# A decoder layer on one core: the held prefetch at the second residual, split first casts, PSUM tiles and stores at the end

## The chip, the cores and the metric

The kernel runs on one core of one Trainium2 chip. The metric is the device time of one execution in microseconds (us). Before the change it is 2006.1 us, the median of three runs between 2005.92 and 2006.18. PE is TensorE, DVE is VectorE, ACT is ScalarE, POOL is GpSimd and SP is SyncE, whose queue issues nearly all DMAs here.

## What is computed

One hybrid decoder layer on 256 tokens of width 2048 in float32: two token mixers side by side (retention and an RG-LRU), merged by gates; cross-attention to 256 memory tokens; a gated FFN of width 5632 with a causal convolution; and a last RMS norm. Cut to the steps around the change:

```python
h = h + merged @ w_mix_out                       # first residual
hn = rmsnorm(h, norm_xa_w)
h = h + memory_cross_attention(hn, mem_n, ...)   # ends with o @ xa_w_o: second residual
hn = rmsnorm(h, norm_ffn_w)
up = causal_dwconv(hn @ ffn_w_up, conv_w, conv_b)
gate, val = jnp.split(up, 2, axis=-1)
h = h + (silu(gate) * val) @ ffn_w_down          # third residual
return rmsnorm(h, final_norm_w)
```

## The kernel before, in words

**Products.** Every float32 product is made of three PE passes over operands that are each split into a rounded part hi and a rest lo (hi x hi, lo x hi, hi x lo). Activations stand by feature in tiles `s` (both parts side by side), so they are PE's stationary operand; weights are the moving operand, 512 columns wide. A product has 16 tiles of 128 rows of weights (k-tiles), taken in chunks of four (KC), and two halves of 128 tokens each. A chunk is thus 4 x 2 x 3 = 24 matmuls of 128x512. PE keeps the order of the program (L221).

**The weight stream.** The host lays all weights out in the order of use. `prefetch(n)` (L237) takes chunks from this stream until n are ahead: it requests a chunk from SP into a tile `raw` (three buffers), ACT casts it to `hi` (L283) and DVE subtracts to get `lo` (L284), two k-tiles at a time, into six buffers each. `chunks` (L296) calls `prefetch(AHEAD)` with AHEAD = 2 after it has taken each chunk, and then runs what `later` has put off by a number of chunks. The tile framework's scheduler then orders the instructions of each engine; what is marked `keep_in_program_order` keeps its place among the marked. The first ten chunks are the interleaved chunks of two products (EARLY = 2, 2, 4, 4, 4 k-tiles each), whose requests are marked. In front of them stand WARM matmuls on a tile of ones (L218).

**Turning rows.** A product gives rows by token, and the next product needs them by feature. `by_dma` (L364) copies rows to 16-bit planes on ACT (L372, one copy for each half of the tokens), turns each with a transposing DMA on SP (L373), and puts off a `join` by some chunks, in which ACT joins the planes again (L383). `split_cols` (L425) then scales by the norm weight and splits into hi and lo (L429 on ACT, L430 on DVE).

**The second residual.** `residual` (L792) makes four column blocks of the product with xa_w_o. The first two are interleaved. For each block DVE adds the accumulator to the rows of h (L804), and `by_dma` turns them (L805), with a wait of one chunk for all but the second. The FFN's first gate product follows at once; its chunk i needs the turned block i.

**The end.** `down` (L949) adds the last FFN product. Its last block goes through `last_down` (L964): the first 128 tokens are made in one accumulator of 512 columns, the second in two pieces of 256 columns, in the unused halves of two accumulator tiles. Each half's sums of squares go to POOL for a power (L998, L1000), then DVE and ACT scale four blocks and four stores of 256 KB each leave, three from SP and one from ACT (L1001 to L1012).

Of the kernel before, what the change touches and what calls it, by code (L numbers as in the profile page):

```python
# [31 lines left out]
RAW_BUFS = 3  # L32
PART_BUFS = 6
AHEAD = 2
WARM = 8
FREE = 300
RG_WAIT = 3
EPS = 1e-6
# [98 lines left out]
def hybrid_layer(  # L137
# [96 lines left out]

    at = [0]

    def prefetch(n):  # L237
        while len(ahead) < n and taken[0] < len(stream):
            i = taken[0]
            name, row, nk, c = stream[i]  # L240
            taken[0] += 1
            size = nk * P * BW
            src = wall[at[0] : at[0] + size].rearrange("(p k n) -> p k n", p=P, k=nk)
            at[0] += size
            if i < 4:
                raw = big([P, KH, BW], s="raw")
            else:
                raw = wp.tile([P, KC, BW], F32, tag="raw", bufs=RAW_BUFS, name=nm("raw"))
            k2 = row // (KH * P)
            early = i < 2 * len(EARLY)  # L250
            own = early and i % 2 == 0
            cuts = range(nk + 1) if i == 0 else range(0, nk + 1, KH) if i < 6 else (0, nk)
            if own:
                xs.load(k2 + 1)
            for a, b in zip(cuts, cuts[1:]):
                load(raw[:, a:b, :], src[:, a:b, :], early)
                if i == 0 and a == 0:
                    load(*xs.rest, early)
                elif own and a == 0:
                    xs.load(k2 + nk // KH)  # L260
            if i >= 6:
                load_x(min(4, 2 * i - 11))
            if i == 8:
                load(cid, consts[:, 0:C_DEC], True)
                load(pa[:, 16:P], by_feature[:, 16:P], True)
                load(pb, by_feature[:, P : P + 80], True)
            if i == 13:
                load(pf.rearrange("p a n -> p (a n)"), by_feature[:, P + 80 :], True)
            if i in (8, 9):
                for b in (2 * i - 16, 2 * i - 15):  # L270
                    sum_squares(xin[b], ss0, b)
            parts = []
            for k in range(0, nk, KH):
                if own:
                    xs[k2 + k // KH]
                hi = wp.tile([P, KH, BW], F32R, tag="hi", bufs=PART_BUFS, name=nm("hi"))
                lo = wp.tile([P, KH, BW], F32R, tag="lo", bufs=PART_BUFS, name=nm("lo"))
                for cs in (slice(k, k + 1), slice(k + 1, k + 2)) if i < 2 else (slice(k, k + KH),):
                    ds = slice(cs.start - k, cs.stop - k)
                    if i == 0:  # L280
                        dve.tensor_copy(hi[:, ds], raw[:, cs, :])
                    else:
                        act.copy(hi[:, ds], raw[:, cs, :])  # L283
                    dve.tensor_tensor(  # L284
                        out=lo[:, ds], in0=raw[:, cs, :], in1=hi[:, ds].bitcast(F32), op=ALU.subtract
                    )
                parts.append((hi, lo))
            ahead.append(((row, c), parts))
# [7 lines left out]
    def chunks(nk, w, row, c):  # L296

        i = gemms[0]
        assert plan[i] == (w, row, nk, c), (i, w, row, nk, c)
        gemms[0] += 1  # L300
        for k, n in pieces(i, nk):
            prefetch(1)
            (r_, c_), parts = ahead.pop(0)
            assert (r_, c_) == (row + k * P, c)
            prefetch(AHEAD)
            yield k, n, parts
            step[0] += 1
            due = [p for p in pending if p[0] <= step[0]]
            pending[:] = [p for p in pending if p[0] > step[0]]
            for _, fn in due:  # L310
                fn()

    def ended(steps):

        for a in steps:
            pass
        return a
# [43 lines left out]

        return t[:, j, cs], t[:, j, S + cs.start : S + cs.stop]

    def by_dma(rows, then, wait=1):  # L364


        planes = big([P, 2, 2, BW], U16, s="pl")
        turned_ = big([P, 2, 4, S], U16, s="pt")
        words = rows.bitcast(U16).rearrange("p t (n h) -> p t h n", h=2)
        for tt in range(2):  # L370
            with tc.high_priority(FREE):
                act.copy(planes[:, tt], words[:, tt])  # L372
            sp.dma_start_transpose(  # L373
                out=turned_.rearrange("p h f s -> p (h f) s")[:, :, tt * P : (tt + 1) * P],
                in_=planes[:, tt].rearrange("p h n -> p (h n)"),
            )

        def join():
            f = big([P, 4, S], s="f")
            halves_ = f.bitcast(U16).rearrange("p f (s h) -> p h f s", h=2)  # L380
            for tt in range(2):
                cs = slice(tt * P, (tt + 1) * P)
                act.copy(halves_[:, :, :, cs], turned_[:, :, :, cs])  # L383
            then(f)

        later(wait, join)
# [405 lines left out]
    def residual(w, st, out, wcol, steps=None):  # L792

        ss = sums()
        products = [steps_n(w, 0, st, NT, b * BW) for b in range(4)]
        for b in range(4):
            if steps:
                steps(b)
            if b == 0:
                for one in products[:2]:  # L800
                    for _ in range(NT // KC - 1):
                        next(one)
            h = hrow[b]
            dve.tensor_add(h, h, ended(products[b]))  # L804
            by_dma(h, lambda f, b=b: turn(f, b, out, wcol), 1 + (b == 1))  # L805
            if b < 2:
                later(2 + b, lambda h=h, b=b: squares(h, ss, b))
            else:
                squares(h, ss, b)
        return ss  # L810
# [153 lines left out]
    def last_down(b0, hid, n, b):  # L964

        h = hrow[b]
        half = sp_.tile([P, 1], F32, tag="half", bufs=1, name="half")
        dve.memset(half, 0.5)
        accs = [acc(), acc()]
        parts = [p for _, _, ps in chunks(n, "ffn_w_down", b0 * BW, b * BW) for p in ps]  # L970

        def total(o, tt, cs):
            for k in range(n):
                hi, lo = (t[:, k % KH, cs] for t in parts[k // KH])
                for _ in products_n(o, hid[k // 2][:, k % 2, :], hi, lo, tt, k == 0, k == n - 1):
                    pass

        for tt in range(2):
            last = big([P, BW + 1], s="last")
            before = sp_.tile([P, 1], F32, tag="pt3", bufs=2, name=nm("pt3"))  # L980
            if tt == 0:
                total(accs[0][:, 0, :], tt, slice(0, BW))
            for c in range(2):
                cs = slice(c * S, (c + 1) * S)
                o = accs[c][:, 1, 0:S] if tt else accs[0][:, 0, cs]
                if tt:
                    total(o, tt, cs)
                y = last[:, c * S : (c + 1) * S + c]
                dve.tensor_add(last[:, cs], h[:, tt, cs], o)  # L989
                junk = tp.tile([P, S + 1], F32, tag="tr", bufs=2, name=nm("junk"))  # L990
                dve.scalar_tensor_tensor(  # L991
                    out=junk[:, 0 : S + c], in0=y, scalar=1.0 / D if c else 1.0, in1=y, op0=ALU.mult, op1=ALU.mult,
                    accum_out=ss3[:, tt, b + c : b + c + 1],
                )
                if c == 0:
                    dve.tensor_reduce(out=before, in_=ss3[:, tt, 0:4], axis=AX.X, op=ALU.add)
                    dve.tensor_scalar_add(before, before, EPS * D)
                    pool.tensor_tensor(out=last[:, BW : BW + 1], in0=before, in1=half, op=ALU.pow)  # L998
            r = sp_.tile([P, 1], F32, tag="ro", bufs=5, name=nm("ro"))
            pool.tensor_tensor(out=r, in0=ss3[:, tt, 4:5], in1=mhalf[:, 0:1], op=ALU.pow)  # L1000
            for c in (1, 0, 3, 2):  # L1001
                y = hrow[c][:, tt, :]
                if c == 3:
                    dve.scalar_tensor_tensor(
                        out=y, in0=last[:, 0:BW], scalar=r, in1=wfin[1][:, 1, :], op0=ALU.mult, op1=ALU.mult
                    )
                elif c == 1:
                    dve.tensor_scalar_mul(y, y, r)
                else:
                    act.mul(y, y, r)  # L1010
                queue = act if c == 2 else sp
                queue.dma_start(out=out[0, tt * P : (tt + 1) * P, c * BW : (c + 1) * BW], in_=y)  # L1012

    ss3 = sp_.tile([P, 2, 5], F32, tag="ss3", bufs=1, name="ss3")

# [60 lines left out]
```

## Time and profile before

| | us |
|---|---|
| median of 3 runs | 2006.1 |
| runs | 2005.92, 2006.10, 2006.18 |
| profiled execution, its own time | 2006.16 |
| its span, first to last instruction | 2004.2 |
| mean granted TensorE clock | 0.999 |

The span of the profiled execution is 1.96 us shorter than its own time; what lies around the span is not on the profile. A row of the timeline has the start from the span's beginning, the time taken, engine and line, the operation, the tiles written and read, and in brackets how long the engine had been idle and what released it. A row of the chain of waits has start, length and what the time went to; "DMA raw<-in_wall" is a weight load under way. "SPq" is the issue of a DMA by SP. The view of windows lists for each stretch the busy time of each engine with its count, then the granted clock, the DMA share and GB/s.

### The profile page before, as it was taken

How to read it: one execution, taken by the hardware profiler on the slowest of the kernel's cores; microseconds unless marked ns; L12 is line 12 of the kernel's file. 1: busy time of each engine (PE TensorE's matmuls, PEld its weight loads, DVE VectorE, ACT ScalarE, POOL GpSimd, SP SyncE). 2: the span in 40 equal slices, each digit the busy share in tenths (PEclk: the TensorE clock that was granted, in tenths of full speed). 3: DMA queues.
4: the chain of work that ended last, by engine and by line, in shares of the span. 5: the costliest groups of instructions: out<-in, count | busy, mean ns of one | idle time of the engine just before them, and what ended most of it. 6: DMA issues, size and time to landing. Idle time of an engine off the chain costs nothing.

```text
span 2004.2 us, 23312 instructions
## 1 busy us (share of the span) xinstructions
PE 1993.6 (99%) x8924; PEld 1656.2 (83%) x8924; DVE 1268.9 (63%) x1566; ACT 1270.2 (63%) x1499; POOL 8.8 (0%) x14
## 2 busy tenths in 40 slices
PE   9999999999999999999999999999999999999998
PEld 7888888888888888888888888888888888888887
DVE  6857756888545555566555654667764576754775
ACT  6646548988444555587666666767763577734763
POOL 0000000000000000000000000000000000000000
PEclk9999999999999999999999999999999999999999
DMA  8755657665655556777666567767665577655673
GB/s 328 238 209 172 237 200 206 214 210 179 218 199 192 199 198 212 268 256 241 203 217 211 193 198 206 213 202 226 231 212 194 179 227 229 204 207 202 205 239 119
DMA packets 197904, 425.58 MB, mean 212 GB/s; under 512 B 142240, under 2 KB 146848, under 8 KB 152736
## 3 DMA queue, kind: packets, MB, share of 16 engines
q1 hardware_dynamic: 197360, 423.55, 64.3%
q8 instruction: 70, 1.15, 0.2%
q10 hardware_dynamic: 432, 0.53, 0.1%
q14 instruction: 42, 0.34, 0.0%
HBM read 388.39 MB, written 2.10 MB: 195 GB/s over the span
## 4 chain that ended last, share of the span: by engine, by line
PE 98%; DMA 1%; DVE 0%; ACT 0%; issue 0%; SPq 0%; POOLq 0%; POOL 0%
PE acc L222 96%; PE sm L222 2%; DMA pt<-pl 0%; DMA raw<-in_wall 0%; DVE lo L284 0%; ACT hi L283 0%; SPq L192 0%; ACT pl L372 0%; ACT nat L1010 0%; DVE last L989 0%; DVE nat L804 0%; ACT junk L822 0%; POOLq L1072 0%; POOL last L998 0%; DVE junk L991 0%
## 5 line engine op out<-in xcount | busy, mean ns | idle before, releaser
L222 PE MATMUL acc<-hi,s 128*128 128x512 f32 x5720 | 1757.7, 389 | 1.2 <-DVE last L989 0.8
L222 PEld LDWEIGHTS acc<-hi,s 128*128 128x128 f32 x5720 | 1071.7, 188 | 222.0 <-DVE last L989 1.3
L284 DVE TENSOR_TENSOR lo<-raw,hi 128x1024 fp32r<-128x1024 f32 (+1 forms) x714 | 859.7, 1220 | 596.9 <-ACT hi L283 579.4
L222 PE MATMUL acc<-lo,s 128*128 128x512 f32 x2860 | 1110.0, 388 | 0.5 <-DVE lo L284 0.5
L283 ACT CAST hi<-raw 128x1024 fp32r<-128x1024 f32 (+1 forms) x712 | 734.5, 1050 | 469.4 <-PE acc L222 427.3
L222 PEld LDWEIGHTS acc<-lo,s 128*128 128x128 f32 x2860 | 537.0, 188 | 112.1 <-DVE lo L284 1.3
L383 ACT COPY f<-pt 128x1024 uint16<-128x1024 uint16 x128 | 168.9, 1353 | 99.9 <-DMA pt<-pl 99.9
L372 ACT COPY pl<-rows 128x1024 uint16<-128x1024 uint16 x100 | 99.7, 1045 | 55.2 <-DVE rows L396 42.9
L396 DVE TENSOR_SCALAR rows<-acc,ro 128x512 f32<-128x512 f32 x76 | 53.4, 744 | 6.2 <-PE acc L222 6.2
L917 DVE SCALAR_TENSOR_TENSOR fg<-f,pf,fg 128x255 f32<-128x255 f32 (+1 forms) x88 | 37.4, 479 | 29.7 <-ACT fg L915 29.3
L917 DVE SCALAR_TENSOR_TENSOR fv<-f,pf,fv 128x255 f32<-128x255 f32 (+1 forms) x88 | 36.1, 478 | 3.9 <-ACT fv L915 3.8
L915 ACT ACTIVATE fg<-f,pf 128x256 f32<-128x256 f32 x44 | 22.9, 592 | 0.3
L915 ACT ACTIVATE fv<-f,pf 128x256 f32<-128x256 f32 x44 | 23.1, 592 | 0.0
L729 DVE SCALAR_TENSOR_TENSOR xr<-f,pa,xr 128x255 f32<-128x255 f32 (+2 forms) x48 | 20.2, 480 | 3.4 <-ACT xr L727 3.3
L404 DVE TENSOR_TENSOR s<-f,s 128x512 fp32r<-128x512 f32 x24 | 15.5, 687 | 9.9 <-ACT s L403 9.9
L430 DVE SCALAR_TENSOR_TENSOR s<-f,pb,s 128x256 fp32r<-128x256 f32 x48 | 20.1, 480 | 2.2 <-ACT s L429 2.2
L372 ACT COPY pl<-nat 128x1024 uint16<-128x1024 uint16 x16 | 15.9, 1045 | 7.5 <-DVE nat L804 7.5
L429 ACT ACTIVATE s<-f,pb 128x256 fp32r<-128x256 f32 x48 | 20.6, 503 | 0.0
L222 PEld LDWEIGHTS sm<-s,s 128*128 128x128 f32 x144 | 18.8, 191 | 0.9
L222 PE MATMUL sm<-s,s 128*128 128x256 f32 (+1 forms) x144 | 18.6, 279 | 0.0
L935 ACT ACTIVATE ft<-fg 128x512 f32<-128x512 f32 x22 | 13.9, 632 | 7.3 <-DVE fg L917 7.3
L418 ACT ACTIVATE v<-acc,ro 128x512 fp32r<-128x512 f32 x16 | 11.0, 686 | 10.2 <-DVE v L419 10.2
(137 smaller groups left out, 561.3 us busy)
## 6 DMA issues: line engine op xcount, KB each, us to landing
raw<-in_wall SPq DMA_DIRECT2D x352, 1024.0 KB, 4.9
nat<-in_x SPq DMA_DIRECT2D x8, 512.0 KB, 8.7
raw<-in_wall SPq DMA_DIRECT2D x7, 512.0 KB, 8.6
pt<-pl SPq DMA_TRANSPOSE x128, 3.3
nat<-in_mem SPq DMA_DIRECT2D x4, 512.0 KB, 8.4
xt<-in_x_t SPq DMA_DIRECT2D x3, 512.0 KB, 10.2
xt<-in_mem_t SPq DMA_DIRECT2D x3, 512.0 KB, 4.9
out<-nat SPq DMA_DIRECT2D x6, 256.0 KB, 2.9
```

Of the source, the lines that this page charges most:

```text
L222: tc.keep_in_program_order(pe.matmul(*a, **k))
L283: act.copy(hi[:, ds], raw[:, cs, :])
L284: dve.tensor_tensor(out=lo[:, ds], in0=raw[:, cs, :], in1=hi[:, ds].bitcast(F32), op=ALU.subtract)
L372: act.copy(planes[:, tt], words[:, tt])
L383: act.copy(halves_[:, :, :, cs], turned_[:, :, :, cs])
L396: dve.tensor_scalar_mul(rows[:, tt, :], a[:, tt, :], r[:, tt : tt + 1])
L404: dve.tensor_tensor(out=t[:, :, S:BW], in0=src, in1=t[:, :, 0:S].bitcast(F32), op=ALU.subtract)
L429: act.activation(t[:, j, 0:S], src[:, j, :], AF.Identity, scale=wcol(j))
L430: dve.scalar_tensor_tensor(out=t[:, j, S:BW], in0=src[:, j, :], scalar=wcol(j), in1=t[:, j, 0:S].bitcast(F32), op0=ALU.mult, op1=ALU.subtract,
L729: dve.scalar_tensor_tensor(out=y[:, s:S], in0=z[:, 0 : S - s], scalar=p_cw(3 - s, t), in1=y[:, s:S], op0=ALU.mult, op1=ALU.add,)
L915: act.activation(y, z[:, j, :], AF.Identity, scale=pf[:, 2, t : t + 1], bias=pf[:, 3, t : t + 1])
L917: dve.scalar_tensor_tensor(out=y[:, s:S], in0=z[:, j, 0 : S - s], scalar=pf[:, 2 - s, t : t + 1], in1=y[:, s:S], op0=ALU.mult, op1=ALU.add,)
```

## The change

There are four edits in one.

1. The start: one warm matmul less; the first weights are requested ahead of the first x; four chunks of the stream instead of two are cast and subtracted one k-tile at a time.
2. The second residual's last block: the chunks up to the last are taken first, then, while `held` is set, the last chunk is taken without a prefetch; its two transposing DMAs are marked to keep their order; then the prefetch runs, its request marked as well.
3. The last product's second half gets two accumulator tiles of its own.
4. The end: the scaling by the last norm weight is taken out of the last step; DVE and ACT write into a tile of 4 x 512 columns, which leaves in two stores of 512 KB from SP.

```diff
-WARM = 8
+WARM = 7
...
+    held = [False]
+
+    def prefetch(n, pin=False):
...
-            if own:
+            if own and i > 0:
                 xs.load(k2 + 1)
             for a, b in zip(cuts, cuts[1:]):
-                load(raw[:, a:b, :], src[:, a:b, :], early)
+                load(raw[:, a:b, :], src[:, a:b, :], early or pin)
                 if i == 0 and a == 0:
+                    xs.load(1)
                     load(*xs.rest, early)
...
-                for cs in (slice(k, k + 1), slice(k + 1, k + 2)) if i < 2 else (slice(k, k + KH),):
+                for cs in (slice(k, k + 1), slice(k + 1, k + 2)) if i < 4 else (slice(k, k + KH),):
...
-            prefetch(AHEAD)
+            if not held[0]:
+                prefetch(AHEAD)
...
-    def by_dma(rows, then, wait=1):
+    def by_dma(rows, then, wait=1, pin=False):
...
-            sp.dma_start_transpose(
+            turning = sp.dma_start_transpose(
...
+            if pin:
+                tc.keep_in_program_order(turning)
...
+            hold = b == 3 and steps is None
+            if hold:
+                for _ in range(NT // KC - 1):
+                    next(products[b])
+            held[0] = hold
             dve.tensor_add(h, h, ended(products[b]))
-            by_dma(h, lambda f, b=b: turn(f, b, out, wcol), 1 + (b == 1))
+            by_dma(h, lambda f, b=b: turn(f, b, out, wcol), 1 + (b == 1), hold)
+            if hold:
+                held[0] = False
+                prefetch(AHEAD, True)
...
-        accs = [acc(), acc()]
+        accs = [acc() for _ in range(3)]
...
-                o = accs[c][:, 1, 0:S] if tt else accs[0][:, 0, cs]
+                o = accs[1 + c][:, 0, 0:S] if tt else accs[0][:, 0, cs]
...
+                dve.tensor_tensor(out=last[:, cs], in0=last[:, cs], in1=wfin[1][:, 1, cs], op=ALU.mult)
             r = sp_.tile([P, 1], F32, tag="ro", bufs=5, name=nm("ro"))
             pool.tensor_tensor(out=r, in0=ss3[:, tt, 4:5], in1=mhalf[:, 0:1], op=ALU.pow)
-            for c in (1, 0, 3, 2):
...
-                queue.dma_start(out=out[0, tt * P : (tt + 1) * P, c * BW : (c + 1) * BW], in_=y)
+            scaled = wp.tile([P, 4, BW], F32, tag="raw", bufs=RAW_BUFS, name=nm("out"))
+            rows = [hrow[c][:, tt, :] for c in range(3)] + [last[:, 0:BW]]
+            for c in range(2):
+                dve.tensor_scalar_mul(scaled[:, 2 * c, :], rows[2 * c], r)
+                late = S if c else 0
+                act.mul(scaled[:, 2 * c + 1, late:], rows[2 * c + 1][:, late:], r)
+                if late:
+                    dve.tensor_scalar_mul(scaled[:, 3, 0:late], rows[3][:, 0:late], r)
+                sp.dma_start(
+                    out=out[0, tt * P : (tt + 1) * P, 2 * c * BW : 2 * (c + 1) * BW],
+                    in_=scaled[:, 2 * c : 2 * c + 2, :].rearrange("p c n -> p (c n)"),
+                )
```

More of the change, by code (lines that the diff above doesn't have):

```diff
@@ L235, in hybrid_layer @@
     at = [0]
-    def prefetch(n):
+    held = [False]
+    def prefetch(n, pin=False):
         while len(ahead) < n and taken[0] < len(stream):
@@ L998, in last_down @@
                     pool.tensor_tensor(out=last[:, BW : BW + 1], in0=before, in1=half, op=ALU.pow)
+                dve.tensor_tensor(out=last[:, cs], in0=last[:, cs], in1=wfin[1][:, 1, cs], op=ALU.mult)
             r = sp_.tile([P, 1], F32, tag="ro", bufs=5, name=nm("ro"))
             pool.tensor_tensor(out=r, in0=ss3[:, tt, 4:5], in1=mhalf[:, 0:1], op=ALU.pow)
-            for c in (1, 0, 3, 2):
[L1002 to L1011, printed above, removed]
-                queue.dma_start(out=out[0, tt * P : (tt + 1) * P, c * BW : (c + 1) * BW], in_=y)
+            scaled = wp.tile([P, 4, BW], F32, tag="raw", bufs=RAW_BUFS, name=nm("out"))
[10 more added lines that the diff above has]
+                )
     ss3 = sp_.tile([P, 2, 5], F32, tag="ss3", bufs=1, name="ss3")
```

## The prediction

> **What bounds the kernel now.** I read the page first, then the waits of PE, then the chain of waits from its end, and last the timeline at the places where the chain leaves PE. Two rows of the page, of its part 1 and its part 4:
>
> ```profile
> PE 1993.6 (99%) x8924; PEld 1656.2 (83%) x8924; DVE 1268.9 (63%) x1566; ACT 1270.2 (63%) x1499; POOL 8.8 (0%) x14
> ...
> PE 98%; DMA 1%; DVE 0%; ACT 0%; issue 0%; SPq 0%; POOLq 0%; POOL 0%
> ```
>
> PE is busy for 99% of the span and carries 98% of the chain, so an edit matters only where PE stands still, before its first matmul or after its last. The change keeps every matmul of the product and their order. The chain of waits shows where PE is left:
>
> ```profile
> 3.55 6.33 DMA raw<-in_wall
> ...
> 9.90 1.06 ACT hi L283
> ...
> 10.98 1.24 DVE lo L284
> ...
> 1112.79 161.66 PE acc L222 x713
> ...
> 1275.55 1.23 DVE lo L284
> 1276.78 1.14 DVE nat L804
> ...
> 1292.92 693.70 PE acc L222 x3059
> ...
> 1987.45 4.58 PE acc L222 x36
> ```
>
> Three places: the start (until 12.3), the end of the second residual (1276 to 1293), and the last product (before 1987.45). The row of 713 matmuls gives the pitch of PE, 161.66/713 = 0.2267 us; a chunk of four k-tiles is 24 matmuls, 5.44 us. The timeline of PE prices the three gaps:
>
> ```profile
> 11.04 0.70 PE L222 MATMUL acc<-hi,s 128*128 128x512 f32 x2
> 12.27 0.50 PE L222 MATMUL acc<-lo,s 128*128 128x512 f32 x1 [0.53 <-DVE lo L284]
> ...
> 1292.17 0.39 PE L222 MATMUL acc<-hi,s 128*128 128x512 f32 x1
> 1292.92 0.50 PE L222 MATMUL acc<-hi,s 128*128 128x512 f32 x1 [0.36 <-DVE s L430]
> 1293.25 0.40 PE L222 MATMUL acc<-lo,s 128*128 128x512 f32 x1
> ...
> 1986.22 0.39 PE L222 MATMUL acc<-lo,s 128*128 128x512 f32 x1
> 1987.45 0.50 PE L222 MATMUL acc<-hi,s 128*128 128x256 f32 x2 [0.84 <-DVE last L989]
> ```
>
> From start to start, less the pitch: two matmuls and a lo from 11.04 to 12.27 should take 0.45 and take 1.23, and the matmul behind the lo starts 0.11 late as well, 0.9 lost. At 1292.17 the next two start 0.52 and 0.10 late, 0.6 lost. At 1986.22 the next starts 1.00 late. So the three edits on PE's path can win 2.5 us together, 0.12%. A measurement of this kernel tells about 0.2%, 4 us, from no change. The question is whether an edit costs PE more than that.
>
> **Part by part.**
>
> *Own PSUM tiles (L969, L985).*
>
> ```profile
> 1986.64 0.75 DVE L989 TENSOR_TENSOR last<-nat,acc 128x256 f32<-128x256 f32 x2 [3.63 <-PE acc L222]
> ```
>
> The second half's first piece goes to another buffer than the one that DVE reads at 1986.64, so the wait <-DVE last goes. Nothing is late next: DVE had been idle for 3.6 us, so it had long read what lay in the second and third buffer. Value -1.0; ends -1.0 and 0 (if the matmuls waited for something else besides).
>
> *Weights first, one warm matmul less, four chunks split (L35, L253, L278).* Splitting the third chunk's cast into single tiles replaces the chain 9.90 to 12.22 (1.05 + 1.23 and hand-overs) by the half shapes, of which the timelines of ACT and DVE have two pairs (ahead of them PE's own beginning):
>
> ```profile
> 1.05 3.78 PE L219 MATMUL warm<-ones 128*128 128x128 f32 x16 [1.05 <-DVE half L968]
> 4.73 1.77 PE L222 MATMUL acc<-hi,s 128*128 128x512 f32 x4
> 6.34 0.62 PE L222 MATMUL acc<-lo,s 128*128 128x512 f32 x2
> 6.79 1.07 PE L222 MATMUL acc<-hi,s 128*128 128x512 f32 x4
> ...
> 7.24 1.15 ACT L283 CAST hi<-raw 128x512 fp32r<-128x512 f32 x2 [2.32 <-DMA raw<-in_wall]
> ...
> 7.90 1.29 DVE L284 TENSOR_TENSOR lo<-raw,hi 128x512 fp32r<-128x512 f32 x2 [0.77 <-ACT hi L283]
> ```
>
> A half cast takes about 0.6 and a half subtraction 0.7. The data still come at 9.88, so the first lo is there at 9.9 + 0.6 + 0.7 = 11.2, ahead of 11.5, where PE wants it; the second lo at 11.9 is ahead of 12.2. Value -0.9. The requests are swapped, not made fewer: the first weights land sooner, the first x later, and both are needed for the first matmul at 4.73. I cost the swap and the missing warm matmul at nothing, because they lie under the cast that waits for the second weights; if PE comes to 11.04 later, that is lost one for one. Ends: -1.1, and +0.8 where the gap behind seven warm matmuls makes the clock come later (fourth rival). The four extra instructions on ACT and on DVE lie in their idle time.
>
> *Stores (L1001 to L1012).* Scaling by the norm weight moves in front of the power, beside POOL; two stores of 512 KB stand for four of 256 KB. DVE's and ACT's last pieces now end about 0.2 sooner, while the first store waits for ACT's 0.7 instead of DVE's 0.5. The bytes are the same.
>
> ```profile
> 1997.99 1.33 ACT L1010 ACTIVATE nat<-nat,ro 128x512 f32<-128x512 f32 x2 [6.62 <-POOL ro L1000]
> ...
> 1998.39 0.75 DVE L1004 SCALAR_TENSOR_TENSOR nat<-last,ro,wf 128x512 f32<-128x512 f32 x1
> ...
> raw<-in_wall SPq DMA_DIRECT2D x352, 1024.0 KB, 4.9
> ...
> out<-nat SPq DMA_DIRECT2D x6, 256.0 KB, 2.9
> ```
>
> No row has a 512 KB store. Value 0; ends -0.4 (the last pieces sooner, fewer requests) and +0.7 (256 KB more behind the last request: (4.9 - 2.9)/3).
>
> *The held prefetch (L802 to L805, L365).* This part decides. For the last block of the second residual the loop no longer prefetches before the block's last chunk; it issues the two transposing DMAs in a pinned order, and only then requests the weights of the FFN gate's second chunk. In the built program SP's order before is transpose, weights, transpose, the gate's second chunk between the two transposes of the third block, its third and fourth behind them; after, it is four transposes (two of the third block, two of the fourth), and then the gate's second, third and fourth chunk. SP issues in order. So loads that stood at 1261.37 and from 1265.55 on are now queued behind two DMAs that wait for the residual's own end. These are the rows that clock it:
>
> ```profile
> 1261.37 0.51 SPq L192 DMA_DIRECT2D raw<-in_wall  x1
> 1265.55 10.17 SPq L192 DMA_DIRECT2D raw<-in_wall  x3
> ...
> 1276.70 1.22 DVE L804 TENSOR_TENSOR nat<-nat,acc 128x1024 f32<-128x1024 f32 x1
> ...
> 1277.94 2.00 ACT L372 COPY pl<-nat 128x1024 uint16<-128x1024 uint16 x2 [1.06 <-DVE nat L804]
> ...
> 1279.02 1.25 SPq L373 DMA_TRANSPOSE pt<-pl  x1
> ...
> 1347.56 2.62 SPq L373 DMA_TRANSPOSE pt<-pl  x2
> 1350.29 1.89 SPq L192 DMA_DIRECT2D raw<-in_wall  x2
> ...
> raw<-in_wall SPq DMA_DIRECT2D x1, 1024.0 KB, 5.0
> ...
> raw<-in_wall SPq DMA_DIRECT2D x1, 1024.0 KB, 5.4
> ```
>
> The last two come from the DMA views of 306.5 to 310 and 168.6 to 172, where a weight load follows two transposes directly, as it will here. Step by step on before's time axis:
> - The gate's fourth chunk starts at 1292.17, so its first starts at 1292.17 - 3 x 5.44 = 1275.85 and its second is due at 1281.29. The second's first lo is due two matmuls later, 1281.75.
> - The residual's last matmul starts at 1275.62. DVE adds 0.42 after the last start (1986.22 to 1986.64); before it was held to 1276.70 by the cast of 1275.55, which after lies behind. So the add starts at 1276.04, 0.66 sooner.
> - Add to copy 1.24, copy to first transpose 1.08, first transpose to weight load 2.73: request at 1281.09.
> - Landing 5.2 later, 1286.29. ACT's cast 1.06: 1287.35. DVE's lo 1.23 and hand-overs: 1288.6.
>
> ACT's order puts the two joins and four scalings of the last block ahead of that cast, but with transposes landing after 3.2 us as at 1347.56 they end at about 1286, beside the load. The third block's joins move ahead of the gate's first chunk's casts as well; that chunk is due at 1275.85, some 5 us later than I find them done.
>
> ```profile
> DMA to landing us min/median/max: 3.2/3.2/3.2
> ```
>
> PE therefore waits from 1281.75 to 1288.6 of its lo: **6.9 us**. The 0.6 of 1292 goes, since the joined rows are ready long before the later fourth chunk. Net +6.3. Behind it nothing is late: the third chunk's load follows the second's back to back. Ends +5.6 (landing 4.7) and +7.0.
>
> *The clock after that wait.* PE does nothing from 1281.5 to 1287.4, 5.9 us, and no gap of before inside the kernel is a fifth of that. Only its end shows what an idle PE does to its clock (windows; the granted clock stands behind the engines, 1.00 and 0.50), and its start, quoted above, how a cold one runs:
>
> ```profile
> 1996.10:1999.40 3.30, 0.24 (x2) 0.03 (x1) 2.00 (x5) 1.33 (x2) 0.55 (x1) 1.00 0.01 6
> 1999.50:2004.20 4.70, 0.00 (x0) 0.00 (x0) 0.00 (x0) 0.00 (x0) 0.00 (x0) 0.50 0.63 211
> ```
>
> The clock was halved between 1999.4 and 1999.5, 3.1 us behind the last matmul's end, so 5.9 us should halve it too. At the start PE works from 1.05, takes (6.34 - 4.73)/4 = 0.40 for a matmul until about 6.1, and then 0.23: 5 us from first work to full speed. Restarting at 1287.4 it would be at half speed until 1292.4; from 1288.6 on that is 3.8 us at 0.40 instead of 0.227 a matmul, 0.43 of the time lost, 1.65. I take 1.7; ends 0 (the clock holds) and 2.4 (5.5 us of it).
> [...]
>
> *Sum.* -1.0 - 0.9 + 0 + 6.3 + 1.7 = +6.1 on the profiled execution's own 2006.16 (span 2004.2 and 1.96 around it), 2012.3. The profiled execution lies 0.06 over the median of 2006.1, so the forecast is **2012.2 us**, 0.30% slower.
>
> **The rivals.**
> 1. *The wait, but the clock holds.* All of the above without 1.7: 2010.5. [...] Against it: the gap is nearly twice the 3.1 us.
> 2. *The weights arrive in time and the transposes' row pays* (the other side, faster). Mechanism: the load of the gate's second chunk is in SBUF when PE comes to it, and the joins of 1281 to 1292 are early. Then -1.0 - 0.9 - 0.6 = 2003.6. It decides by the request: a lo at 1281.75 needs the weights at 1279.4 and the request at 1274.2, before the residual's last matmul. For it: DMA engines are idle enough. Against it: SP's order, and a transpose that cannot be issued before the add.
> 3. *The edits at the edges do nothing* (the PSUM wait stays, the start is bound by landing times), while PE's wait is as above: 2014.1.
> 4. *The warm-up is broken.* Seven warm matmuls end 0.45 sooner; the gap before the first product delays full clock by some 3 us. Matmuls at 0.40 until 9 or so cost up to 1.2, and the 0.9 is lost: 2013.1 to 2014.3.
>
> **How the numbers follow.** Forecast 0.66 (alone 2011.2 to 2013.2), rival 1 0.15, rival 2 0.06, rivals 3 and 4 0.05 and 0.08. The range 2009.6 to 2014.2 takes in rival 1 with its shortest landing and most of 3 and 4; it leaves out rival 2 and tails, 0.15. More than 0.2% slower is above 2010.1: the forecast, 3, 4, and most of rival 1, together 0.86. Within 0.2%: the rest of rival 1, 0.08. Faster: rival 2, 0.06.
>
> **What would show it.** Right: a PE gap of 5 to 6 us to the first hi of the gate's second chunk and a second one of about 1.2 to its lo, released by ACT hi and DVE lo behind a DMA raw<-in_wall; a granted clock of 0.5 within some 6 us of it; no wait on DVE last at the end; no gap at 12.27. Wrong: SP's weight load issued ahead of the last transposes, or PE without a gap there; then the time is 2003 to 2004. If the clock stays at 1.00, rival 1 holds. If PE's first chunk starts late or its pitch stays at 0.4 beyond 6.1, rival 4 does.

## The result and the profile after

The changed kernel takes 2013.06 us, the median of six runs (2012.24 to 2013.90), beside 2006.10 (2005.92 to 2006.25). The ratio is 1.0035, with a 95% interval of 1.0023 to 1.0047: slower, by more than the 0.2% that counts as a difference here. The forecast was 2012.2 in 2009.6 to 2014.2. The profiled execution took 2012.24 us with a span of 2010.46 (printed 2010.5), 6.24 more than before's 2004.22 (printed 2004.2); 1.78 lies around the span.

The page of the changed kernel, the row of engines from its part 1, the first row of its part 4 and one of its part 6:

```profile
PE 1994.7 (99%) x8922; PEld 1656.0 (82%) x8922; DVE 1270.4 (63%) x1574; ACT 1268.8 (63%) x1501; POOL 9.3 (0%) x14
...
PE 98%; DMA 0%; DVE 0%; ACT 0%; issue 0%; POOL 0%; SPq 0%; POOLq 0%; DVEq 0%; ACTq 0%
...
out<-out SPq DMA_DIRECT2D x4, 512.0 KB, 3.1
```

None of these rows shows the loss: PE is still at 99% and has 98% of the chain, because 6 us are 0.3%. The stores are four of 512 KB, landing in 3.1 us. The waits of PE show it at once, before and then in the changed kernel (what PE waited for, total, times, longest):

```profile
PE warm L219 <- DVE half L968: 1.1, 1, 1.1
PE acc L222 <- DVE last L989: 0.8, 1, 0.8
PE acc L222 <- DVE lo L284: 0.5, 1, 0.5
PE acc L222 <- DVE s L430: 0.4, 1, 0.4
```

```profile
PE acc L222 <- ACT hi L286: 5.8, 1, 5.8
PE warm L219 <- DVE half L982: 1.1, 1, 1.1
PE acc L222 <- ACT s L435: 0.5, 1, 0.5
PE acc L222 <- DVE hi L284: 0.5, 1, 0.5
PE acc L222 <- DVE s L436: 0.2, 1, 0.2
```

The new one is a single wait, for one cast; the next longest is the first warm matmul's, at the start. The chain of waits of the changed kernel tells what stands behind it, start and length:

```profile
1276.23 1.23 DVE nat L815
...
1277.48 2.00 ACT pl L376 x2
1279.48 1.25 ACT junk L836 x4
...
1281.27 5.00 DMA raw<-in_wall
...
1286.35 1.05 ACT hi L286
...
1288.71 705.47 PE acc L222 x3106
...
1994.20 0.75 DVE last L1003 x2
```

Before, too, the chain left PE, from 1274.44 to 1292.92, but only because it follows back what released the one matmul that came late at 1292.92; PE itself worked for 18.12 of these 18.48 us. Now the chain leaves PE at 1276.21 and goes through the residual's add, the copies to planes, the time in which SP issues the last transpose (the chain names ACT's sums of squares, which run beside it), and a whole weight load and its cast before PE has work again. SP's part of the timeline says why the load starts so late:

```profile
1257.33 0.33 SPq L192 DMA_DIRECT2D raw<-in_wall  x1
1260.67 20.50 SPq L377 DMA_TRANSPOSE pt<-pl  x4
1281.27 17.23 SPq L192 DMA_DIRECT2D raw<-in_wall  x7
```

Four transposes stand in a row for 20.5 us, two of them waiting for the last block's add, and no weight load gets past them. Before, loads left SP at 1261.37 and from 1265.55 on. PE's timeline and the windows of the changed kernel show what that costs:

```profile
1281.24 0.39 PE L222 MATMUL acc<-lo,s 128*128 128x512 f32 x1
1287.44 1.22 PE L222 MATMUL acc<-hi,s 128*128 128x512 f32 x2 [5.81 <-ACT hi L286]
1288.71 0.79 PE L222 MATMUL acc<-lo,s 128*128 128x512 f32 x1
1289.30 1.05 PE L222 MATMUL acc<-hi,s 128*128 128x512 f32 x2
1290.15 0.63 PE L222 MATMUL acc<-lo,s 128*128 128x512 f32 x1
1290.58 0.88 PE L222 MATMUL acc<-hi,s 128*128 128x512 f32 x2
```

```profile
1284.40:1291.00 6.60, 3.51 (x7) 2.32 (x8) 5.12 (x7) 5.69 (x8) 0.00 (x0) 0.50 1.01 402
1291.20:1300.00 8.80, 8.80 (x41) 7.23 (x40) 5.80 (x5) 4.99 (x5) 0.00 (x0) 1.00 0.93 364
```

PE stops for 5.8 us and restarts at a granted clock of 0.50, at which three matmuls from 1289.30 to 1290.58 have a pitch of 0.427 us; the clock is 1.00 again from 1291.2 on. The trace's record of the clock has the half clock from 1284.30 to 1291.12, 6.83 us.

**Where the time went.** Four places of each trace cut its span into stretches that belong to one edit each: PE's first matmul into a tile `sm` (the start ends there), DVE's first add into `last` (the middle, with the second residual), PE's last matmul (PSUM tiles) and the end of the span (stores). In the timelines the first two stand like this, for before and then for the changed kernel (before's add is quoted in the prediction):

```profile
142.51 0.80 PE L222 MATMUL sm<-s,s 128*128 128x256 f32 x6
```

```profile
142.69 0.80 PE L222 MATMUL sm<-s,s 128*128 128x256 f32 x6
...
1994.20 0.75 DVE L1003 TENSOR_TENSOR last<-nat,acc 128x256 f32<-128x256 f32 x2 [3.92 <-PE acc L222]
```

This table has all kernels of the study, with the time (median) beside the stretches of the one profiled execution. "Hold" is edit 2.

| kernel | time | start | middle | PSUM tail | end |
|---|---|---|---|---|---|
| before | 2006.10 | 142.51 | 1844.13 | 9.42 | 8.16 |
| changed | 2013.06 | 142.69 | 1851.51 | 8.32 | 7.94 |
| e1 changed, no hold | 2004.97 | 143.86 | 1843.46 | 8.32 | 7.81 |
| e2 before, hold alone | 2014.52 | 142.90 | 1851.45 | 9.43 | 8.15 |
| e3 changed, three ahead | 2006.04 | 142.50 | 1845.33 | 8.31 | 7.95 |
| e4 changed, matmuls in the gap | 2011.41 | 143.09 | 1850.43 | 8.31 | 7.80 |
| e5 before, split alone | 2005.30 | 142.61 | 1843.46 | 9.43 | 8.17 |
| e6 before, order alone | 2006.44 | 143.08 | 1843.46 | 9.41 | 8.16 |
| e7 before, PSUM tiles alone | 2005.02 | 143.90 | 1843.47 | 8.31 | 8.19 |
| e8 before, stores alone | 2005.66 | 143.01 | 1843.46 | 9.41 | 7.95 |
| e9 before, seven warm alone | 2006.22 | 143.29 | 1843.46 | 9.43 | 8.31 |
| e10 changed, no hold, eight warm | 2004.04 | 142.69 | 1843.46 | 8.31 | 7.80 |
| e11 changed, eight warm | 2012.83 | 142.50 | 1852.44 | 8.31 | 7.79 |
| e12 before, three winning parts | 2003.95 | 142.54 | 1843.47 | 8.31 | 7.80 |

The first two rows differ by +0.18 + 7.38 - 1.10 - 0.22 = +6.24, the whole of the span's growth. Read by columns, tail and end fall into two groups each, by their edit, within 0.2 us. The middle is 1843.46 or 1843.47 wherever the hold is off, but for before's own execution. The start scatters by 1.4 us.

### The profile page after: what moved, and what is told of

It reads as the page before. It is cut to its first block, busy times and chain, and to the rows that moved or that the text cites. A ratio compares the mean times of both kernels' runs of the same rounds, so it can differ in the third digit from the quotient of the medians.

```text
span 2010.5 us, 23310 instructions
## 1 busy us (share of the span) xinstructions
PE 1994.7 (99%) x8922; PEld 1656.0 (82%) x8922; DVE 1270.4 (63%) x1574; ACT 1268.8 (63%) x1501; POOL 9.3 (0%) x14
## 3 DMA queue, kind: packets, MB, share of 16 engines
q8 instruction: 69, 1.13, 0.2%
## 4 chain that ended last, share of the span: by engine, by line
PE 98%; DMA 0%; DVE 0%; ACT 0%; issue 0%; POOL 0%; SPq 0%; POOLq 0%; DVEq 0%; ACTq 0%
PE acc L222 96%; PE sm L222 2%; DMA raw<-in_wall 0%; ACT pl L376 0%; DVE out L1019 0%; SPq L192 0%; ACT junk L836 0%; DVE nat L815 0%; DVE last L1003 0%; POOL last L1012 0%; ACT hi L286 0%; POOLq L1087 0%; DVE junk L1005 0%; POOL ro L1015 0%; DVE last L1013 0%
```

## The experiments

Theory: the held prefetch puts the request of the gate's second chunk behind transposes that wait for the residual's end, so PE waits 7 us and then works for a while at half clock; the other edits win 1 to 2 us together. Rivals: the loss comes from the other edits (start, stores), or the wait costs what it does without the clock.

**e1: the hold undone, all else as changed.**

```diff
-            hold = b == 3 and steps is None
+            hold = False
```

> All of the change but the held prefetch and the pinned order (the flag is never set). Theory (the held prefetch makes PE wait for the gate's second chunk): no PE gap at 1281, the gaps of 1292 return (0.6 us), and what the edges give is left: 2006.1 - 1.1 (PSUM) - 0.2 (stores) + 0.2 (start, as in the changed kernel's trace) = 2005.0; 2003.9 if the start's late landings there were chance. Rival (the loss sits in another edit): at or above 2009.

Measured: 2004.97 (2003.90 to 2009.07, 11 runs) beside 2005.95, ratio 0.9996 (0.9987 to 1.0005). The chain of waits of this kernel has no stop between the last matmuls into `sm` and the tail:

```profile
1111.27 2.87 PE sm L222 x24
1114.14 873.16 PE acc L222 x3852
```

One piece of 3852 matmuls covers the place where the changed kernel stops. The hold thus costs 2013.06 - 2004.97 = 8.1 us, more than the changed kernel's whole loss of 7.0. The expectation that the short stops of 1292 would be back failed: they are not here either.

**e2: the hold alone on the kernel before** (the `held`, `pin` and `hold` lines of the diff above, nothing else).

> The kernel before with the held prefetch and the pinned order alone. Theory: PE's lo of the gate's second chunk waits 6.8 us, the clock falls to 0.5 and costs 1 to 2 us, the 0.6 us of 1292 goes: 2006.1 + 7.4 = 2013.5 (2012.5 to 2014.5). Rival (the loss needs another edit, such as the pinned loads of the start): 2005.5 to 2006.5.

Measured: 2014.52 (2013.84 to 2014.99, 4 runs), ratio 1.0042 (1.0028 to 1.0056): 8.6 us over before's 2005.95, a middle of 1851.45, 7.99 over the 1843.46 that eight kernels without the hold share. PE's timeline repeats the changed kernel's:

```profile
1281.45 0.39 PE L222 MATMUL acc<-lo,s 128*128 128x512 f32 x1
1287.73 1.22 PE L222 MATMUL acc<-hi,s 128*128 128x512 f32 x2 [5.89 <-ACT hi L285]
```

The hold alone makes the whole stop; the other edits have no part in it. The rival of the other edits falls.

**e3: the hold kept, but three chunks requested ahead of it.**

```diff
             if hold:
+                prefetch(AHEAD + 1)
                 for _ in range(NT // KC - 1):
                     next(products[b])
...
-                prefetch(AHEAD, True)
+                prefetch(AHEAD + 1, True)
```

> The changed kernel, with three chunks instead of two prefetched before the hold and after it: the gate's second chunk is requested in time, its third behind the transposes. Theory (the wait is the distance between request and need): the third chunk's lo, ready at 1288.7 as the second's was, is due at 1287.4, so PE waits 1.3 us instead of 6.8 and the clock holds: 2006.1 + 0.2 - 1.1 - 0.2 - 0.6 + 1.3 = 2005.7 (2005 to 2006.5). Rival (four transposes ahead of the loads cost by themselves, whichever chunk is late): above 2009.

Measured: 2006.04 (2005.62 to 2007.14, 11 runs), ratio 1.0001 (0.9992 to 1.0010). SP's and PE's rows in this kernel's timeline, the first three of SP's:

```profile
1260.34 1.25 SPq L377 DMA_TRANSPOSE pt<-pl  x1
1261.69 0.52 SPq L192 DMA_DIRECT2D raw<-in_wall  x1
1262.26 18.73 SPq L377 DMA_TRANSPOSE pt<-pl  x3
...
1287.65 0.73 PE L222 MATMUL acc<-hi,s 128*128 128x512 f32 x2 [0.76 <-ACT hi L286]
1288.91 0.50 PE L222 MATMUL acc<-lo,s 128*128 128x512 f32 x1 [0.53 <-DVE lo L287]
```

The second chunk's load passes at 1261.69 as it did before, PE runs on through 1281, and the stop moves to the third chunk, which still queues behind the transposes: 0.76 and 0.53 in place of 5.81, and no half clock. The transposes stand in the same kind of row and cost nothing by themselves: PE loses 0.92, 0.81 and 0.10 at the three starts behind 1286.50, 1287.65 and 1288.91, and that is all but 0.04 of the 1.87 by which the middle lies over 1843.46. What costs is the one load that they hold back, and even so the hold wins nothing. The hold without the pinned order was not run; what the pinning alone does stays open.

**e4: idle matmuls in the gap**, 26 of 128x128 on the tile of ones between the gate's first and second chunk (two records each in the trace).

```diff
+            if step[0] == filler[0]:
+                fill = px.tile([P, 2, S], F32, tag="sm", name="fill")
+                for _ in range(26):
+                    mm(fill[:, 0, 0:P], ones, ones, start=True, stop=True)
```

> The changed kernel with 26 idle matmuls on a tile of ones put between the gate's first and second chunk, some 5.5 us of PE work that nobody reads, inside the wait. Theory (part of the loss is the halved clock after the wait): the granted clock stays at 1.00, PE's lo comes at the same 1288.7, and the time falls by 1.2 to 2 us to 2011.5, with runs closer together than 2012.2 to 2013.9. Rival (the wait is all, the clock costs nothing): 2013.

Measured: 2011.41 (2010.62 to 2012.08, 7 runs), ratio 1.0027 (1.0016 to 1.0038), 1.65 under the changed kernel. PE's timeline and the same windows:

```profile
1281.88 5.97 PE L222 MATMUL fill<-ones 128*128 128x128 f32 x52
1287.88 0.73 PE L222 MATMUL acc<-hi,s 128*128 128x512 f32 x2
...
1289.47 0.63 PE L222 MATMUL acc<-hi,s 128*128 128x512 f32 x2
```

```profile
1284.40:1291.00 6.60, 6.04 (x41) 5.10 (x41) 4.60 (x7) 5.68 (x9) 0.00 (x0) 1.00 1.00 415
```

PE is idle no more, though it does nothing of use, the clock stays at 1.00, and two matmuls behind the wait take 0.63 instead of 1.05. The load is as late as ever: its first lo reaches PE at 1289.14, and without the 0.40 by which this execution's start is later, that is 1288.74 against 1288.71. So the wait and the clock are two costs, and the clock's is 1.65 by the medians and 1.08 by the middles (1851.51 - 1850.43). The rival without the clock falls, too.

**e5 to e8: the other parts, each alone on the kernel before.** The start's gain had not come in the profile (+0.18), and the raw tiles had landed about 1.1 us later than before. Was it the order of requests, or chance?

```diff
# e5: split alone
-                for cs in (slice(k, k + 1), slice(k + 1, k + 2)) if i < 2 else (slice(k, k + KH),):
+                for cs in (slice(k, k + 1), slice(k + 1, k + 2)) if i < 4 else (slice(k, k + KH),):
# e6: order of the first requests alone
-            if own:
+            if own and i > 0:
...
+                    xs.load(1)
# e7: PSUM tiles alone
-        accs = [acc(), acc()]
+        accs = [acc() for _ in range(3)]
...
-                o = accs[c][:, 1, 0:S] if tt else accs[0][:, 0, cs]
+                o = accs[1 + c][:, 0, 0:S] if tt else accs[0][:, 0, cs]
# e8: the last scaling and the stores alone, as in the change
```

> The kernel before with one part of the start alone: the third and fourth chunk's high and low parts are made tile by tile; the order of the first requests, eight warm matmuls and everything else stay. Theory A (the split takes the 0.93 us gap of TensorE at the third chunk away, and the late landings of the changed kernel come from the order of its requests): TensorE's first matmul of the second stage at about 141.6 where before has 142.5, landings of the first loads as in before, a time of about 2005.1, 0.9 under before. Theory B (the landings are late because the split brings requests closer, or by chance of the execution): the landings come about 1 us later as they do in the changed kernel, the first matmul of the second stage stays near 142.5, a time of about 2006.1.

> The kernel before with the other part of the start alone: the first weights are requested ahead of the first piece of the input; no split, eight warm matmuls, nothing else changed. Theory A (the order makes the landings late): the second weight lands about 1 us later than before's 5.95 us, TensorE's first matmul of the second stage is 0.5 to 1.1 us later, at 143.0 to 143.6, a time of 2006.6 to 2007.2. Theory B (landings vary from execution to execution, the order does nothing): within 0.3 us of before, 2005.8 to 2006.4, and the landings as in before or spread at random.

> The kernel before with one change alone: the last pieces accumulate in PSUM tiles of their own. Theory A (the pieces waited for VectorE to read the tile, the changed kernel's tail shows 1.10 us less between the second residual's last product and the last matmul): TensorE's 1.2 us gap near 1986 is gone, and the time falls by 1.0 to 1.1, to 2005.0. Theory B (the tail is then bound by VectorE's last adds, the gap only moves): 2005.8 to 2006.1.

> The kernel before with the last scaling and the stores of the changed kernel alone: two stores of 4 KB rows in place of four of 2 KB for each half, and VectorE multiplies by the last weight before the scale is known. Theory A (what the changed kernel's profile shows: the last landing 0.49 us earlier after the scale is ready, the scale's power on GpSimd 0.23 us longer beside VectorE's added multiply): 0.2 to 0.3 us less from the last matmul to the end, 2005.7 to 2005.9. Theory B (the power's longer time is chance): 0.5 less, 2005.5. In both the power's row in the profile tells: 0.78 for A, 0.55 for B.

Measured beside a common 2006.32 (33 runs), 11 runs each: split 2005.30, ratio 0.9996 (0.9987 to 1.0005); order 2006.44, 1.0001 (0.9992 to 1.0009); PSUM 2005.02, 0.9994 (0.9985 to 1.0003); stores 2005.66, 0.9996 (0.9987 to 1.0005). Each interval holds 1, so the times alone settle none of them; the stretches do for two. Every kernel with PSUM tiles of their own has a tail of 8.31 or 8.32, every one without 9.41 to 9.43: 1.1 us. With the new stores the end is 7.79 to 7.95, without them 8.15 to 8.31: 0.2 to 0.5 us.

At the start it was chance, not the order of requests. The third load of weights landed at 8.31 in the changed kernel, at 7.22 in before and 7.57 in e2, but at 8.50 in e7 and 8.12 in e9, whose requests are in the very same order, and at 7.55 in e6, where the order is the new one. Over all fourteen executions it lands between 7.22 and 8.50 with the old order and between 7.55 and 8.31 with the new. Without an edit of the start (before, e2, e7, e8) it ends at 142.51, 142.90, 143.90 and 143.01; before's profiled execution is the best of the four, and it was the yardstick of the prediction.

**e9 to e12: the seventh warm matmul, and the parts together.** e1 has split, PSUM tiles and stores, yet won only 1.0, where the singles add up to -1.0 + 0.1 - 1.3 - 0.7 = -2.9. PE's rows at the start of e1:

```profile
1.05 3.35 PE L219 MATMUL warm<-ones 128*128 128x128 f32 x14 [1.05 <-DVE half L982]
4.92 2.30 PE L222 MATMUL acc<-hi,s 128*128 128x512 f32 x4 [0.52 <-ACT s L435]
```

Seven leave a hole of 0.5 us ahead of the first product. In the windows of e1 and then of e10, its twin with eight, whose hole is 0.14, the next 3.3 us look like this:

```profile
7.30:10.60 3.30, 3.30 (x9) 2.51 (x9) 2.39 (x6) 2.05 (x4) 0.00 (x0) 1.00 0.96 346
```

```profile
7.30:10.60 3.30, 3.26 (x13) 2.11 (x13) 2.26 (x4) 2.05 (x4) 0.00 (x0) 1.00 0.96 342
```

PE is busy throughout in both, with 9 matmuls in e1 (0.37 each) and 13 in e10 (0.25 each): e1's PE still runs slowly. The printed clock has no record that early and shows 1.00; the first record comes at 10.66 in e1 and at 6.73 in e10.

```diff
# e9: before      e10: changed, no hold      e11: changed
-WARM = 8
+WARM = 7
# (e10 and e11 the other way round)
```

> The kernel before with seven warm matmuls in place of eight, nothing else. In the kernels with seven, the warm matmuls end at 4.41 and the first product starts near 4.95, so TensorE idles for 0.55 us; with eight it idles for 0.1 or less. [...] Theory B (the kernel waits for its loads at that time anyway, so the clock costs nothing): 2006.0 to 2006.4, as my prediction had it when it put the seventh warm matmul at nothing.

> The changed kernel without the held prefetch and with eight warm matmuls; its twin with seven had 2004.97. Theory A (the missing warm matmul gave back what split, PSUM tiles and stores won): clock granted by 7.9 us, 2003.5 to 2003.9, near the sum of the single parts, 2006.3 - 1.0 + 0.1 - 1.3 - 0.7 = 2003.4. Theory B: 2004.8 to 2005.2, as with seven.

> The changed kernel with eight warm matmuls, nothing else. Theory A: 1.2 to 1.5 us less than with seven, 2011.6 to 2011.9, and less spread between executions. Theory B: 2012.8 to 2013.2 as with seven.

> The kernel before with the three parts that won alone: PSUM tiles of their own, the four chunks split, the last scaling and stores; without the held prefetch, the order of the first requests and the seventh warm matmul as before. If the parts add up: 2006.3 - 1.3 - 1.0 - 0.7 = 2003.3; by the segments of the profiles alone, 2006.3 - 1.1 - 0.6 - 0.2 = 2004.4. If their order of first requests mattered, this is 0.1 to 0.3 under the changed kernel without its hold and with eight warm matmuls.

Measured beside 2006.12 (27 runs): e9 2006.22, 1.0001 (0.9992 to 1.0009); e10 2004.04, 0.9990 (0.9981 to 0.9999); e11 2012.83, 1.0033 (1.0021 to 1.0046); e12 2003.95, 0.9990 (0.9981 to 0.9999). The eighth warm matmul is worth 0.9 in e10 against e1, but 0.1 in e9 against before and 0.2 in e11 against the changed kernel. Theory A of e10 and e11 is thus not borne out in size. In e9's profiled execution the clock was up at 4.00, and its runs reach from 2005.15 to 2008.72 where before's end at 2007.19 beside it (at 2007.74 beside e5 to e8), as one would expect if the hole costs something in some executions only. Split and eight warm matmuls together (e5, e10, e11, e12) start within 142.50 to 142.69; split with seven (changed, e1, e3, e4) within 142.50 to 143.86. The first record of the full clock comes between 4.29 and 6.73 in all nine executions with eight; in the five with seven it comes at 4.00, 4.30 and 4.78, but at 8.88 in e4 and 10.66 in e1. How much the seventh costs on average stays open between 0.1 and 0.9 us.

e12 is the best kernel of the study with e10: 2.2 and 2.1 us under before, 0.10%. Its chain has the piece of 873.16 us and 3852 matmuls of e1, too.

The expected 2003.3 from the single medians was 0.65 too low and 2004.4 from the stretches 0.45 too high; the order of the first requests is worth nothing that shows (2003.95 and 2004.04).

## Why the prediction was right, and where it was not

- **The held prefetch** carried the forecast and was right in mechanism and size. The wait of PE from the time at which it is due for the second chunk's first lo was put at 6.9; on the changed trace it is due at 1281.24 + 3 x 0.2267 = 1281.92 and comes at 1288.71, 6.8. Request, landing, hi and lo were put at 1281.09, 1286.29, 1287.35 and 1288.6, and the chain above has 1281.27, 1286.27, 1287.40 and, by the matmul that waits for it, 1288.7. e2 shows that the edit does it alone. One of the signs did not come as described: the second gap, for the lo, is not among the waits of PE, because the row of the two hi matmuls before it, at half clock, reaches from 1287.44 to 1288.66. With the clock up, in e3 and e4, such a gap shows as 0.53.
- **The 0.6 at 1292** was credited as a gain, and before's trace loses it: 1844.13 - 1843.46 = 0.67. But none of the eight other kernels without the hold has those stops, six of them with the second residual's code unchanged and two with the hold switched off. In before's execution the second of the last block's joins on ACT began 7.98 us after SP issued the last transpose; in those eight it was 5.99 to 6.61. The stop belonged to one execution, and the forecast should have counted nothing for it: the hold costs 8.0 to 9.0 by the middles and 8.1 to 8.8 by the medians (e1, e2, e10 and e11), where the prediction had 6.3 + 1.7 = 8.0 net. A stop seen in one profile was taken for a property of the kernel. That the changed kernel's profiled execution has just these 8.0 (1851.51 - 1843.46 = 8.05) is in part luck: 0.6 too much was credited, and the cost of the clock was put 0.6 too high (next point).
- **The halved clock** came as forecast, though not its size. 1.7 was taken; the profile has 1.08 against e4, the medians 1.65. But e11 has the half clock from 1285.69 to 1292.52, 1.4 us later, while its PE restarts at 1287.64, 0.2 later: (1292.52 - 1288.90) x 0.47 = 1.7 (the share of time lost is 1 - 0.2267/0.427 = 0.47), where the changed kernel's profiled execution has (1291.12 - 1288.71) x 0.47 = 1.1. So both prices occur, by when the half clock, 6.83 us long in both, happens to begin.
- **The start: this step failed.** It was put at -0.9, and the profile has +0.18. The split did what was worked out: no wait on a lo of the third chunk is left among the waits of PE, and with eight warm matmuls the start is within 0.2 us of before's best. What failed is the step "the data still come at 9.88". ACT's cast that waits for these data shows it, before and then in the changed kernel:

```profile
9.90 1.05 ACT L283 CAST hi<-raw 128x1024 fp32r<-128x1024 f32 x1 [0.40 <-DMA raw<-in_wall]
```

```profile
11.03 2.39 ACT L286 CAST hi<-raw 128x512 fp32r<-128x512 f32 x4 [0.41 <-DMA raw<-in_wall]
```

  It starts 1.13 later, which eats up the 0.9 won, and in no other kernel of the study does it start before 10.27. Among the four kernels whose start is the same code (before, e2, e7, e8) it starts between 9.90 and 11.28, so 142.51 was a lucky yardstick. That before's own time still lay 0.06 from its median is luck again: the early start and the stop of 0.67 about cancel. And the missing warm matmul, costed at nothing, leaves a hole behind which full clock can come late, as my fourth rival had it with some 3 us: in e1 its first record is at 10.66, 3.93 later than in e10, while e9, with 4.00, shows that it doesn't come every time.
- **PSUM tiles**: -1.0 forecast, -1.10 measured, the same in every kernel that has them. After the add of 1994.20 no row of PE waits for DVE `last`.
- **Stores**: 0 forecast, -0.22 measured, of two parts, as the next rows show. Before's timeline, then the changed kernel's, at the last power on POOL:

```profile
1997.41 0.55 POOL L1000 TENSOR_TENSOR ro<-ss,mhalf 128x1 f32<-128x1 f32 x1 [3.33 <-DVE junk L991]
```

```profile
2000.78 0.54 POOL L1012 TENSOR_TENSOR last<-pt,half 128x1 f32<-128x1 f32 x1 [2.78 <-DVE pt L1011]
...
2003.83 0.42 DVE L1013 TENSOR_TENSOR last<-last,wf 128x256 f32<-128x256 f32 x1
2003.87 0.78 POOL L1015 TENSOR_TENSOR ro<-ss,mhalf 128x1 f32<-128x1 f32 x1 [2.56 <-DVE junk L1005]
```

The power takes 0.23 longer now that DVE multiplies beside it, and what follows is 0.45 shorter. The multiply that the change put "beside POOL" was priced as if it were free there.

In sum, the median lies 0.9 over the forecast, nearly all of it from the start: by e1 the hold costs 8.1 where 8.0 was put, and the other edits win 1.0 where 1.9 was put.

## What to carry to other kernels

Before holding back a prefetch, follow the queue's order. Here a load stood behind transposes that waited for computed data (SP's row of 20.50 us), left at 1281.27, and its landing of 5.00 and cast of 1.05 fell on PE, which stopped for 5.81; one load more ahead of the hold took 7 of the 8 us away. In this kernel, whose PE is 99% busy, the edges are worth about 2 us in 2006 while one stop inside costs 8, so ask first whether any edit can make PE stop. And look at a stop of half a microsecond in more than one execution before you count on winning it.

## What the hardware showed unexpectedly

- POOL's power on 128x1 took 0.54 to 0.56 us with DVE idle and 0.78 to 0.80 beside DVE's 128x256 TENSOR_TENSOR, in the changed kernel, e8 and e12 alike.
- The clock rises at times that vary from execution to execution (first record between 4.00 and 10.66 us), while in the changed kernel's trace its later changes lie whole multiples of one length apart: 4.30, 1284.30, 1291.12 and 2007.92 are 1280.00, 6.83 and 716.80 us apart, and with half of the 6.83, 3.413, as the unit that is 375, 2 and 210.
